# Delta-rule step: reordering the products with the state and sharing one PSUM bank between outputs and update

## The chip, the cores and the metric

The kernel runs on one core of one Trainium2 chip. The metric is the device time in microseconds of one execution; the number given for a kernel is the median of its runs.

## What is computed

The reference is two blocks of two transformer layers each, on 512 tokens of 1024 features, the second block with 256 context tokens beside them. The first layer of the second block has, next to an attention with low-rank keys and values (MLA), a gated delta-rule recurrence of 8 heads with 64 features each. It goes over chunks of 64 tokens in both directions. The preparation of a chunk gives `u`, `w`, `qk`, `q_dec`, `k_dec` and the decay `g_last`; then the state `s` (64 x 64 for each head) is carried from chunk to chunk:

```
def step(s, inp):
    u_i, w_i, qk_i, qd_i, kd_i, gl_i = inp
    v_new = u_i - jnp.einsum('bhck,bhkv->bhcv', w_i, s)
    o_i = jnp.einsum('bhck,bhkv->bhcv', qd_i, s) + jnp.einsum('bhcs,bhsv->bhcv', qk_i, v_new)
    s = s * gl_i[..., None, None] + jnp.einsum('bhck,bhcv->bhkv', kd_i, v_new)
    return s, o_i
```

All of this is in float32. The sequence has 4 + 8 chunks (context, then tokens), so there are 12 chunks in each of two directions.

## The kernel before, in words

The whole of both blocks is one program for one core. Weights come from DRAM in units of 128 output features, are split into two float32r parts (`hl`, L397) and multiplied in three passes (`mm3`, L411 to L417). That is most of the time and is not touched.

The change lies in the stage marked "gdn" (L1792 to L1818). `gdn_scan` (L1518) runs six walks (`walk`, L1624). A walk calls `solve` (L1524) once for each direction, which prepares a block of 128 tokens (two chunks), and then `step` (L1583) four times: two chunks, and for each both directions in turn. So there are 24 steps. Between the walks, and before the first one, units of the MLA attention are traced (`mla`, L1378, by the counts in `UNITS`, L288): scores `S` (L1400), their maxima and exponentials (`soft_rows`, L1320), transpositions `ptr` (L1346) and products with the values `po` (L1363).

The framework that the kernel is written in orders the instructions of each engine itself: it takes what was traced first among what is ready by its own model, and it writes all semaphores. So the order in the trace is not the order of the source; work of the attention and of the next `solve` fills TensorE's places while a step waits for VectorE. An engine then runs its list strictly in that order. The framework keeps two engines that use one PSUM bank of a tile apart in time.

A step, with `rows` the 64 partitions of its chunk:

- L1586 to L1588: four products `ws` = w times state (`wT`, `St`), into a PSUM tile of the ring "step". This ring has a single bank (`MIXERS`, L289), so every PSUM tile of a step waits until the one before it has been read.
- L1589 and L1590: VectorE makes `vn` = u - ws.
- L1591 to L1597: the outputs `ot`, in a new tile of the same ring. For each of the four pairs of heads one product of the state with `qd` (stationary operand 128 x 128, 64 columns) and then, added to it, one product of `vn` with `qk` for each of the two heads (64 x 64, 64 columns).
- L1598 to L1604: the outputs go to `oT`: ScalarE copies them where this chunk is seen for the first time (L1603), VectorE adds them where the other direction has been there (L1601).
- L1605 to L1608: the update `up`, in a third tile of the ring: eight products of `kd` and `vn` (64 x 64, 64 columns).
- L1609 to L1615: VectorE, for each half of the partitions, multiplies the state by its decay (L1614) and adds the update (L1615).

A float32 product shows in the trace as two matmuls, each with a weight load of its own: 8 for `ws`, 8 and 16 for `ot`, 16 for `up` in each step.

Of the kernel before, what the change touches and what calls it, by code (L numbers as in the profile page):

```python
# [26 lines left out]
class Cols:  # L27
    """Names columns of a packed [128, n] array."""
# [17 lines left out]
def units(w, m=128):  # L46
    """[K, N] -> [N/m, 128, K/128 * m]: one weight unit after the other, each contiguous per partition."""
    k, n = w.shape
    return np.ascontiguousarray(w.reshape(k // 128, 128, n // m, m).transpose(2, 1, 0, 3)).reshape(n // m, 128, -1)


def chunk_units(w, sizes):
    """[K, N], K cut into chunks of sizes*128 -> flat array of units (chunk, n): [128, size*128] each."""
    out, k0 = [], 0
    for s in sizes:
        out.append(units(w[k0:k0 + s * 128]).reshape(-1))
        k0 += s * 128
    return np.concatenate(out)
# [26 lines left out]
def chunk_constants():  # L85
    """Masks of chunks of 64 tokens, two chunks on 128 partitions."""
# [45 lines left out]
def na_bias(rpb):  # L132
    """rpb laid out over [query in block, 256 context keys and the block's local keys]; NEG outside the window."""
# [18 lines left out]
def prepare(x):  # L152
    """Lays the inputs out: feature-major activations, weights in units, vectors as columns."""
# [85 lines left out]
def build(tc, A, out, cst_at, vec_at, chk_at, tap=None, upto=99, mark=lambda n: None):  # L239
# [16 lines left out]
    def store(dst, src):  # L256
        """apart from the loads, which it would hold back while it waits"""
        nc.gpsimd.dma_start(dst, src)
# [48 lines left out]
    # ---- scratch, by block  # L307
# [3 lines left out]
    def scr(tag, cols=512):  # L311
        """nt, sq: for the products; ct, cs: for the norms of parts that run beside"""
        p, w = state["sp"] if tag in ("nt", "sq") else (state["np"], {tag: 256})
        return p.tile([128, w[tag]], F32, name=tag, tag=tag, bufs=2 if tag == "sq" else 3)[:, :cols]
# [14 lines left out]
    # ---- background work: the adaLN products, a unit after each unit of weights  # L329
# [9 lines left out]
    # ---- the norms of a part of the tokens, which go along with the products of the next one  # L339
# [15 lines left out]
    def settle(sl=None):  # L355
        """all that the tokens wait for"""
# [3 lines left out]
    def release():  # L360
        """what reads the last products"""
        while pending and not pending[-1][2]:
            advance()

    # ---- weights: a raw unit, its float32r head and its rest
# [12 lines left out]
    # the units in the order of their use, each made two units before it  # L378
# [3 lines left out]
    def plan(seq):  # L382
        """Units to come: (src, tiles, place or None, key), or the key of a unit made before, which still lies there"""
        coming.extend(seq)
# [16 lines left out]
    # ---- activations in two parts: h(p, k, tokens) is feature tile k of the head (p = 0) or the rest  # L401
# [9 lines left out]
    def mm3(jobs, kt=8, first=True, last=True, k0=0):  # L411
        """jobs: (ps, (H, L), activations, tokens); ps += sum_k W[k]^T h[k0 + k], in three float32r passes, k outermost"""
# [6 lines left out]
    def unit_on(kt, h, sls, src=None):  # L419
        """One unit of weights times the token slices: a bank each."""  # L420
# [7 lines left out]
    def linear(units_, h, sls, groups, evac, skew=0, kt=8, stay=3):  # L428
        """Plans the units, returns the run: evac(i, tokens, ps) for each unit; the first `skew` units go group of parts
        by group, so that a part whose input comes late doesn't hold the others; the last units of a group (stay) serve  # L430
        the next one too"""
# [14 lines left out]
        def early(n):  # L446
            """the products of the first n steps, whose places come later"""
# [14 lines left out]
    def places(p, n, kt=8):  # L462
        """n places for weights that stay, in pool p"""
        return [[p.tile([128, kt, 128], F32R, name=f"keep{i}{q}") for q in "HL"] for i in range(n)]

    def out_linear(srcs, h, parts, evac, after, keep=(), lead=1):
        """Plans the units, returns the run: part by part, all the output tiles: evac(n, tokens, ps), then after(tokens).
        srcs[n]: the units of output tile n along the contraction, [(src, tiles)].
        Units with a place of their own (keep) are made once, as are the last ones of a part for the next part.
        lead: so many output tiles at first go along the contraction together"""  # L470
# [38 lines left out]
    # ---- norms over the features (partitions and tiles)  # L509
    def add_square(acc, v, tag="sq"):  # L510
        """acc[0] (+)= v^2"""
# [9 lines left out]
    def rsqrt_cols(sqs, ns, n, off, ring="ax", p=None):  # L521
        """1/sqrt(sum over 128/ns partitions / n + off): tokens on the partitions, a column for each of their blocks and sums"""
# [10 lines left out]
    def rsqrt_steps(sq, n, out):  # L533
        """rsqrt_bc(sq, 1, n) in steps, appended to out"""
# [4 lines left out]
    def on_features(rs, ns, ws, ring="ax"):  # L539
        """such columns on the partitions of their features again: in PSUM, in parts of the widths ws"""  # L540
# [17 lines left out]
    def modulated(xk, rs, a, b, h, sl, ks=range(KD)):  # L558
        """h (in two parts) = x * rs * a + b"""
# [7 lines left out]
    # ---- softplus of a small array  # L567
# [16 lines left out]
    # ---- adaLN: products along the free axis, one output feature per partition  # L584
# [22 lines left out]
    # ======== block 1 ========  # L607
# [15 lines left out]
    def x_plus(gate, acc):  # L623
        """x[n] += gate[n] * ps, and the squares of the sum"""
# [36 lines left out]
    # ---- layer 0: RG-LRU  # L661
    def rglru(after, acc):
        m = mod[0]
        with ExitStack() as st:
# [7 lines left out]
            def yLt(n, dt=F32R):  # L672
                """the rests of block n of y; other things lie there before"""
# [12 lines left out]
            # the first units go along with the modulation of the feature tiles; weights of some lie where y will be  # L686
# [44 lines left out]
            # the steps, by block of features; the gates' units come late, beside the recurrences  # L731
# [35 lines left out]
            def head(n):  # L767
                """the gates of the recurrence; its input lies where y's rest will be"""
# [49 lines left out]
    # ---- layer 1: DSA  # L818
    def stack(dst, p, v, sl):
        """A pair of heads of 64 features: the head and the rest of each on all partitions, as units 2p and 2p + 1"""  # L820
# [6 lines left out]
    def stacked(ps, q, kHL, sl):  # L827
        """q k of such units: k in two parts, each on both halves of the partitions"""
# [3 lines left out]
    def dsa(h, after, acc):  # L832
        m = mod[1]
        with ExitStack() as st:
# [34 lines left out]
            def evac(i, sl, ps):  # L869
# [22 lines left out]
                else:  # L892
# [3 lines left out]
                    # 1 / sqrt(64 (mean square + eps)): the norm and the scale of the scores  # L896
# [6 lines left out]
            def index(b):  # L903
                """the 128 best keys of each query of block b"""
# [35 lines left out]
            def weights(b, g, Ps):  # L940
                """the softmax of the heads of group g, query block b"""
# [52 lines left out]
            def o(p, k, sl):  # L994
                """the output lies where its queries were"""
# [35 lines left out]
    def chain(name, g, sc, sh):  # L1031
        """The next norm's input, made part by part as x is finished."""
# [41 lines left out]
    # ======== block 2 ========  # L1074
# [18 lines left out]
    def grid(v, n=8):  # L1093
        """tokens row by row of the grid, as (row, column) of a tile that goes column by column"""
# [11 lines left out]
    def decay_logs(stack):  # L1106
        """lg: log decay and log beta; egc, kdw: exp of the decays' sums along the chunks, from both ends"""
# [25 lines left out]
    # ---- the products of the even mixer's input: all that the mixers need goes to DRAM  # L1133
    def even_in(h, beside):
        """beside: called after the products that it needs, returns functions to run one by one between the others"""
        with ExitStack() as st:
# [73 lines left out]
            def conv(i):  # L1210
# [23 lines left out]
                # the norms of some units together, for the sake of the tables of functions  # L1234
# [17 lines left out]
            def stored(i, c):  # L1252
                """tokens on the partitions"""
# [65 lines left out]
    # ---- softmax over the free axis, and the products with the values  # L1319
    def soft_rows(Ps, scores, scale, mx, rsum):  # L1320
        """P = exp(scale * (S - max S)), and its sums; scores(i): S of row i in PSUM, in pieces side by side"""
# [13 lines left out]
    def weigh(po, Ps, keys, vals, tp, ring):  # L1335
        """po[64 * half:, (i, q)] = sum over key tiles j of V^T P[half][i]^T; keys[j]: the keys of each i, [(first, number)];
        vals(half, j): V, or V for each i"""
# [84 lines left out]
    def off_diagonal(d, a):  # L1422
        """rows and columns of the block of NT off the diagonal, of chunk a"""
# [4 lines left out]
    def gdn_chunks(gp, slots):  # L1428
        """The inverses of the chunks' triangles, q k with decays to DRAM: a list of functions to run in order.
        slots: 7 tiles of [128, 32, 32]"""  # L1430
# [13 lines left out]
        def decays(b):  # L1444
            """NT[s, h, c] = k_s k_c beta_s decay(s -> c) within chunks, and q_c k_s likewise, of both directions"""
# [43 lines left out]
        def triangles(key, A):  # L1489
            """1 + A = the transpose of a diagonal 32-block of 1 + N, or itself, so that A is an upper triangle;  # L1490
            every block on its own partition."""
# [4 lines left out]
        def invert(key, A, X, Y):  # L1496
            """Y: the inverses, with the row of the block on the partitions, the block of tokens on their quadrant"""
# [20 lines left out]
    def gdn_scan(oT, gA, gp, beside, then):  # L1518
# [5 lines left out]
        def solve(d, b):  # L1524
            """u = T v, w = T (k exp(g)) of both chunks of a block of 128 tokens; T beta is the chunk's inverse"""
# [13 lines left out]
            # the block off the diagonal, of the inverse of [[1 + N1, 0], [N, 1 + N2]]: -(1 + N2)^-1 N (1 + N1)^-1, transposed  # L1539
# [43 lines left out]
        def step(d, b, a, St):  # L1583
# [7 lines left out]
            po = bank("step", 256, "ot")  # L1591
            for p in range(4):
                o = po[:, 64 * p:64 * p + 64]
                T.matmul(o, St[:, p], qd[:, p, rows], start=True, stop=False)  # L1594
                for half in range(2):
                    h = 2 * p + half
                    T.matmul(o[64 * half:64 * half + 64], vn[rows, h], qk[rows, 64 * h:64 * h + 64], start=False, stop=True)  # L1597
# [7 lines left out]
            pu = bank("step", 256, "up")  # L1605
            for h in range(8):
# [551 lines left out]
```

## Time and profile before

| | us |
|---|---|
| timed runs | 3346.09, 3351.06, 3357.49 |
| median of the runs | 3351.06 |
| span of the profiled execution, first to last instruction | 3335.9 |
| TensorE busy in it | 3192.8 (96%) |
| VectorE busy in it | 2066.5 (62%) |
| ScalarE busy in it | 1470.4 (44%) |
| gdn stage in it, about | 1545 to 1895 from the start |

The profiled execution has a span alone; what lies around it is read from the median, 3351.06 - 3335.9 = 15.2 us. In all tables PE is TensorE's matmuls, PEld its weight loads, DVE VectorE, ACT ScalarE, POOL GpSimd, SP the queue of the DMAs. "x16" is a count of instructions. L1608 is a line of the kernel. In a timeline, successive instructions of one kind are merged in one row; its duration goes to the modelled end of the last, so what a run takes of TensorE's time is read from its start to the next row's start.

### The profile page before, as it was taken

How to read it: one execution, taken by the hardware profiler on the slowest of the kernel's cores; microseconds unless marked ns; L12 is line 12 of the kernel's file. 1: busy time of each engine (PE TensorE's matmuls, PEld its weight loads, DVE VectorE, ACT ScalarE, POOL GpSimd, SP SyncE). 2: the span in 40 equal slices, each digit the busy share in tenths (PEclk: the TensorE clock that was granted, in tenths of full speed). 3: DMA queues.
4: the chain of work that ended last, by engine and by line, in shares of the span. 5: the costliest groups of instructions: out<-in, count | busy, mean ns of one | idle time of the engine just before them, and what ended most of it. 6: DMA issues, size and time to landing. Idle time of an engine off the chain costs nothing.

```text
span 3335.9 us, 50730 instructions
## 1 busy us (share of the span) xinstructions
PE 3192.8 (96%) x20270; PEld 2686.0 (81%) x20270; DVE 2066.5 (62%) x4067; ACT 1470.4 (44%) x2638; POOL 17.4 (1%) x47
## 2 busy tenths in 40 slices
PE   6999999989999999988999999999997999999998
PEld 5788888965988889866677799888887877798887
DVE  7976555798787787677756575442228446573335
ACT  4955333457443335476343463212125445563222
POOL 0000000000000000000000000000000000000000
PEclk9999999989999999998889999999998999999999
DMA  7556664310365554333122333532213221143323
GB/s 237 183 156 211 194 190 157 107 51 26 103 212 192 190 198 135 117 127 107 48 64 82 105 108 108 158 127 84 68 62 117 84 89 44 58 139 103 99 97 102
DMA packets 137614, 403.58 MB, mean 121 GB/s; under 512 B 13856, under 2 KB 37152, under 8 KB 136736
## 3 DMA queue, kind: packets, MB, share of 16 engines
q1 hardware_dynamic: 135344, 389.32, 36.5%
q0 software_dynamic: 2032, 11.01, 1.0%
q8 instruction: 159, 2.61, 0.3%
q14 instruction: 79, 0.65, 0.1%
HBM read 375.63 MB, written 24.64 MB: 120 GB/s over the span
## 4 chain that ended last, share of the span: by engine, by line
PE 71%; DVE 6%; ACT 3%; issue 1%; DMA 0%; DVEq 0%; ACTq 0%
PE mm L416 51%; PE ptr L1346 2%; PE po L1363 2%; PE rb L547 2%; PE S L1400 2%; PE S L830 1%; PE ss L527 1%; PE ot L1594 1%; PE ot L1597 1%; PE sa L1560 1%; PE ws L1588 1%; PE po L969 1%; ACT wH L398 1%; PE ptr L975 1%; DVE acc L519 1%
## 5 line engine op out<-in xcount | busy, mean ns | idle before, releaser
L398 ACT CAST wH<-raw 128x1024 fp32r<-128x1024 f32 (+4 forms) x446 | 451.9, 1015 | 1149.7 <-PE mm L416 797.9
L399 DVE TENSOR_TENSOR wL<-raw,wH 128x1024 fp32r<-128x1024 f32 (+4 forms) x446 | 525.0, 1179 | 372.6 <-ACT wH L398 365.8
L416 PE MATMUL mm<-mH,wH 128*128 128x256 f32 (+1 forms) x1280 | 407.3, 340 | 9.1 <-DVE f L1747 5.9
L416 PE MATMUL mm<-mH,wL 128*128 128x256 f32 (+1 forms) x1280 | 404.6, 339 | 1.4 <-DVE wL L399 1.4
L416 PE MATMUL mm<-mL,wH 128*128 128x256 f32 (+1 forms) x1280 | 404.8, 339 | 0.0
L589 DVE SCALAR_TENSOR_TENSOR raw<-raw,cond_c 128x1024 f32<-128x1024 f32 x128 | 156.5, 1224 | 176.2 <-DMA raw<-in_ada 175.7
L416 PEld LDWEIGHTS mm<-mH,wH 128*128 128x128 f32 x1280 | 231.3, 190 | 40.2 <-ACT wH L398 6.6
L416 PEld LDWEIGHTS mm<-mH,wL 128*128 128x128 f32 x1280 | 230.4, 190 | 30.4 <-DVE wL L399 1.8
L416 PEld LDWEIGHTS mm<-mL,wH 128*128 128x128 f32 x1280 | 230.9, 190 | 28.5
L416 PE MATMUL mm<-f2u0L,wH 128*128 128x512 f32 (+1 forms) x752 | 190.3, 327 | 0.0
L416 PE MATMUL mm<-f2u0H,wH 128*128 128x512 f32 (+1 forms) x752 | 190.0, 326 | 0.0
L416 PE MATMUL mm<-f2u0H,wL 128*128 128x512 f32 (+1 forms) x752 | 189.6, 326 | 0.0
L416 PE MATMUL mm<-f2u1H,wL 128*128 128x512 f32 (+1 forms) x432 | 151.4, 352 | 1.2 <-DVE wL L399 1.1
L416 PE MATMUL mm<-f2u1H,wH 128*128 128x512 f32 (+1 forms) x432 | 150.9, 352 | 0.6 <-ACT nt L1722 0.5
L416 PE MATMUL mm<-f2u1L,wH 128*128 128x512 f32 (+1 forms) x432 | 151.2, 352 | 0.2
L416 PEld LDWEIGHTS mm<-f2u0H,wL 128*128 128x128 f32 x752 | 118.1, 189 | 13.1
L416 PEld LDWEIGHTS mm<-f2u0H,wH 128*128 128x128 f32 x752 | 117.7, 189 | 12.9
L416 PEld LDWEIGHTS mm<-f2u0L,wH 128*128 128x128 f32 x752 | 117.7, 189 | 12.6
L1727 DVE TENSOR_TENSOR nt<-nt,mm 128x512 f32<-128x512 f32 (+1 forms) x52 | 31.4, 605 | 145.9 <-PE mm L416 145.5
L626 DVE SCALAR_TENSOR_TENSOR x<-mm,mod,x 128x256 f32<-128x256 f32 (+1 forms) x112 | 66.0, 596 | 78.7 <-PE mm L416 78.5
L416 PE MATMUL mm<-f0H,wH 128*128 128x512 f32 (+1 forms) x296 | 107.2, 363 | 0.0
L416 PE MATMUL mm<-f0L,wH 128*128 128x512 f32 (+1 forms) x296 | 107.0, 362 | 0.0
(692 smaller groups left out, 7488.2 us busy)
## 6 DMA issues: line engine op xcount, KB each, us to landing
raw<-in_ada SPq DMA_DIRECT2D x192, 512.0 KB, 3.7
raw<-in_fw SPq DMA_DIRECT2D x142, 512.0 KB, 4.2
raw<-in_gw SPq DMA_DIRECT2D x113, 512.0 KB, 3.3
raw<-in_gw SPq DMA_DIRECT2D x34, 384.0 KB, 3.0
raw<-in_owin SPq DMA_DIRECT2D x25, 512.0 KB, 3.3
raw<-in_ewin SPq DMA_DIRECT2D x22, 512.0 KB, 3.5
raw<-in_awin SPq DMA_DIRECT2D x20, 512.0 KB, 3.7
raw<-in_ewout SPq DMA_DIRECT2D x18, 512.0 KB, 4.1
```

What stands on the lines that cost most here:

```text
L398: S.copy(H, src)
L399: V.tensor_tensor(L, src, H.bitcast(F32), OP.subtract)
L416: T.matmul(ps, W[w][:, k], h(p, k0 + k, sl), start=first and k == 0 and j == 0, stop=last and k == kt - 1 and j == 2)
L519: V.tensor_tensor(acc[0], acc[0], sq, OP.add)
L527: T.matmul(pc[:, ns * b:ns * b + ns], sq, sel, start=True, stop=True)
L547: T.matmul(pb[r * i:r * i + r, b:b + 128], rs[:, c:c + 1].to_broadcast([128, r]), ident, start=True, stop=True)
L589: V.scalar_tensor_tensor(junk, r, 1.0, c, OP.mult, OP.mult, accum_out=o[:, j:j + 1])
L626: V.scalar_tensor_tensor(x[:, n, sl], ps, gate[:, n:n + 1], x[:, n, sl], OP.mult, OP.add)
L830: T.matmul(ps, q, k[:, sl], start=j == 0, stop=j == 1)
L1346: T.transpose(pt[:kn, c:c + 128], Ps[half][i][:, k0:k0 + kn], ident)
L1363: T.matmul(po[r], vs, PT[:kn, half * w:half * w + w], start=j == 0, stop=j == len(keys) - 1)
L1400: T.matmul(pS, q, KQ[half][:, 0, k0 + c0:k0 + c1], start=True, stop=True)
```

## The change

Within `step`, `ot` and `up` become one tile `ou` of the ring "step": its first 256 columns are `po`, the last 256 `pu`. Its 20 products follow one another: the four of the state and `qd`; the eight of the update; the eight of `qk`. A first product alone has the start flag, which clears the bank for all of them. The outputs are read after the last product, and the two operations of VectorE on the state follow as before. The rest of the diff removes comments and docstrings.

```diff
             vn = gp.tile([128, 8, 64], F32, name="vn", bufs=3)
             V.tensor_tensor(vn[rows], u[rows], pw[rows].rearrange("p (h c) -> p h c", h=8), OP.subtract)
-            po = bank("step", 256, "ot")
+
+            ou = bank("step", 512, "ou")
+            po, pu = ou[:, :256], ou[:, 256:]
             for p in range(4):
-                o = po[:, 64 * p:64 * p + 64]
-                T.matmul(o, St[:, p], qd[:, p, rows], start=True, stop=False)
-                for half in range(2):
-                    h = 2 * p + half
-                    T.matmul(o[64 * half:64 * half + 64], vn[rows, h], qk[rows, 64 * h:64 * h + 64], start=False, stop=True)
+                T.matmul(po[:, 64 * p:64 * p + 64], St[:, p], qd[:, p, rows], start=p == 0, stop=False)
+            for h in range(8):
+                r = slice(64 * (h % 2), 64 * (h % 2) + 64)
+                T.matmul(pu[r, 64 * (h // 2):64 * (h // 2) + 64], kd[rows, h], vn[rows, h], start=False, stop=False)
+            for h in range(8):
+                r = slice(64 * (h % 2), 64 * (h % 2) + 64)
+                T.matmul(po[r, 64 * (h // 2):64 * (h // 2) + 64], vn[rows, h], qk[rows, 64 * h:64 * h + 64],
+                         start=False, stop=h > 5)
             ot = oT[:, :, 128 * b + 64 * a:128 * b + 64 * a + 64]
             o3 = po.rearrange("p (i t) -> p i t", i=4)
             if (b, a) in seen:
...
                 S.copy(ot, o3)
                 seen.add((b, a))
-            pu = bank("step", 256, "up")
-            for h in range(8):
-                r = slice(64 * (h % 2), 64 * (h % 2) + 64)
-                T.matmul(pu[r, 64 * (h // 2):64 * (h // 2) + 64], kd[rows, h], vn[rows, h], start=True, stop=True)
             last = 64 * a + (63 if d == 0 else 0)
             p3 = pu.rearrange("p (i t) -> p i t", i=4)
             for half in range(2):
```

## Rows read from the trace of the kernel before

**Rows 1.** The chain that ended last, by line, from 1500 to 2100 us.
```profile
by line: PE mm L416 30.4%; PE S L1400 9.8%; PE po L1363 6.1%; PE ptr L1346 6.0%; PE ot L1594 5.7%; PE ot L1597 4.6%; PE sa L1560 4.2%; PE ws L1588 4.2%; PE rb L547 2.9%; PE up L1608 2.9%; PE gg L1550 2.5%; PE nd L1547 2.4%; PE eg L1573 1.9%
```

**Rows 2.** Busy time of each engine by stretch; the stage is the last row.
```profile
core 0: us, PE busy (x) PEld busy (x) DVE busy (x) ACT busy (x) POOL busy (x), PEclk, DMA share, GB/s
1545.00:1600.00 55.00, 51.21 (x478) 38.89 (x478) 38.30 (x124) 28.79 (x61) 0.71 (x2) 0.83 0.24 75
...
1650.00:1700.00 50.00, 46.91 (x348) 31.70 (x348) 27.96 (x73) 21.71 (x43) 1.07 (x2) 0.66 0.16 42
1700.00:1750.00 50.00, 50.00 (x458) 37.09 (x456) 25.90 (x72) 21.77 (x47) 1.64 (x3) 0.90 0.25 70
...
1800.00:1850.00 50.00, 50.00 (x513) 37.60 (x513) 26.06 (x71) 16.70 (x40) 0.56 (x1) 0.97 0.10 30
1850.00:1900.00 50.00, 47.28 (x409) 32.99 (x407) 26.80 (x64) 16.32 (x29) 1.09 (x2) 0.97 0.29 101
1545.00:1900.00 355.00, 342.07 (x3154) 247.50 (x3154) 214.49 (x595) 145.66 (x307) 8.82 (x17) 0.89 0.23 70
```

**Rows 3.** Timeline of TensorE: the products of one step, from 1732 us.
```profile
1732.44 0.43 PE L1594 MATMUL ot<-qd,St 128*128 128x64 f32 x2
1732.80 0.33 PE L1597 MATMUL ot<-qk,vn 64*64 64x64 f32 x4
1733.06 0.43 PE L1594 MATMUL ot<-qd,St 128*128 128x64 f32 x2
...
1734.94 0.43 PE L547 MATMUL rb<-cst,rsum 128*64 128x128 f32 x2
...
1736.37 0.68 PE L1608 MATMUL up<-vn,kd 64*64 64x64 f32 x16
1736.98 0.66 PE L1346 MATMUL ptr<-cst,P 128*128 128x128 f32 x4
```

**Rows 4.** The same timeline: runs of 128x128 stationary operands, and 512-column products.
```profile
1738.19 1.12 PE L1400 MATMUL S<-kq 96*128 96x512 f32 x2
1739.24 0.69 PE L1550 MATMUL gg<-DT,ND 32*32 32x32 f32 x16
...
1743.10 1.38 PE L1560 MATMUL sa<-VK,DT 128*128 128x128 f32 x10
1744.32 0.95 PE L527 MATMUL ss<-cst,sq 128*128 128x2 f32 x8
1745.13 0.42 PE L1566 MATMUL wt<-cst,w__15727 128*128 128x128 f32 x2
```

**Rows 5.** Waits at line L1608: what ended TensorE's idle time before it.
```profile
  issue: 3.6, 10
  DVE St L1614: 2.8, 4
  ACT oT L1603: 1.4, 3
```

**Rows 6.** VectorE's group of the state's decay, 1545 to 1895 us; its idle time last.
```profile
L1614 DVE TENSOR_TENSOR St<-St,eb 64x256 f32<-64x256 f32 x48 | 20.1, 419 | 39.1 <-PE ot L1594 38.3
```

**Rows 7.** The two readers of the outputs: durations (min/median/max, ns) and counts.
```profile
L1601 DVE TENSOR_TENSOR oT<-ot,oT x12: 386/410/425, 1638.1 to 1878.7; 128x256 f32<-128x256 f32 x12
L1603 ACT COPY oT<-ot x12: 367/372/373, 1570.4 to 1786.1; 128x256 f32<-128x256 f32 x12
```

**Rows 8.** Line L1563, ScalarE's reads of a bank that VectorE reads too: its waits.
```profile
  DVE u L1562: 17.4, 16
```

**Rows 9.** Timeline, all engines: the end of updates and the start of a next step.
```profile
1650.07 0.43 DVE L1615 TENSOR_TENSOR St<-up,St 64x256 f32<-64x256 f32 x1
...
1650.61 0.97 PEld L1588 LDWEIGHTS ws<-St,wT 128*64 128x64 f32 x8
...
1737.10 0.88 DVE L1615 TENSOR_TENSOR St<-up,St 64x256 f32<-64x256 f32 x2 [0.19 <-PE up L1608]
```

**Rows 10.** TensorE's group of `ws`, 1545 to 1895 us; its idle time last.
```profile
L1588 PE MATMUL ws<-St,wT 128*64 128x128 f32 x192 | 30.0, 303 | 1.3 <-DVE St L1615 1.1
```

## The prediction

> **What bounds the kernel now.** I read the chain of waits first, for the 600 us around the changed code [rows 1]. It runs almost wholly over TensorE, and the three lines of the step that the change touches hold 5.7 + 4.6 + 2.9 = 13.2% of it, about 79 us. The reader should see that the chain goes through these products at every step, so time saved in them is on the path as long as TensorE stays the engine that ends the stage. Next the busy time by stretch [rows 2]: in the stage of 355 us TensorE is idle for 13 us; from 1700 to 1850 us it has no idle time (two of the three slices stand in the rows; the third reads the same), while VectorE is busy for half of it and ScalarE for less. Before 1700 there are holes of 3 to 4 us in a slice of 50. The granted clock is 0.89 over the stage, a mixture of 2.4 and 1.2 GHz, lowest (0.66) in 1650 to 1700. So this is a TensorE-bound stage with a step chain threaded through it, and the questions are how much of TensorE's time the new order gives back, and whether the single PSUM bank of the step makes a new wait.
>
> **The change, part by part.**
>
> *Order of the products.* Today the 8 matmuls on `qd` and the 16 on `qk` alternate, 2 and 4 at a time, in four rounds. In a step without a hole at full clock [rows 3] they take 1732.44 to 1734.94 = 2.50 us. A round is 0.36 us for two `qd` matmuls up to the start of the next row, and 0.26 for four `qk` matmuls. The update, 16 matmuls of the same small form, takes 1736.37 to 1736.98 = 0.61 us. Four small ones cost 0.26, sixteen cost 0.61: each costs (0.61 - 0.26) / 12 = 0.029, and leaving the run costs 0.26 - 4 x 0.029 = 0.14. Each round pays this exit, and the update pays it once more. After the change 32 small matmuls stand in one run: 32 x 0.029 + 0.14 = 1.07 us.
>
> For eight `qd` matmuls in one run the trace has no row. The nearest is `sa`, with the same 128 x 128 stationary operand: ten in 1743.10 to 1744.32, so 0.122 us each [rows 4]. I take 8 x 0.122 = 0.98 us. Its moving operand is 128 columns and not 64, so it should rather be too dear. The bound below is `ss`, with 2 columns: eight in 0.81 us, 0.101 each. The bound above is that nothing is gained: 4 x 0.36 = 1.44 us.
>
> Together a step's products behind `vn` cost 2.50 + 0.61 = 3.11 us now and 0.98 + 1.07 = 2.05 after: 1.06 us less. With 24 steps that is 25.4 us at full clock, and at the stage's mean clock of 0.89 about 28.5 us. With the bounds: 24 x (3.11 - 2.51) / 0.89 = 16 us, and 24 x (3.11 - 1.88) / 0.89 = 33 us.
>
> *One PSUM tile fewer.* The update no longer waits for the outputs to be read. TensorE's loads sat idle before L1608 for 3.6, 2.8 and 1.4 us in the largest three entries [rows 5], 7.8 us in all. Part of this is only the loads, behind matmuls still running. I take 0 for it and keep 8 us as the further bound.
>
> *Waits moved.* The multiplication of the state by its decay (L1614) needs the last `qd` product. Today that stands near the end of `ot`, and VectorE sits 39 us idle in front of it [rows 6]; in the new order it is free after 1 us and lies beside the 1.07 us of small products (two operations of 0.42). Cost 0; if it came late it would delay the adds by 0.84. The adds (L1615) now wait for the last `qk` product and for the reader of the outputs, since the bank is shared. In 12 steps this reader is VectorE itself, ahead of them in its queue; in the other 12 it is ScalarE's copy of 0.37 us [rows 7]. While VectorE waits there, the attention's maxima and its copies of `ptr` queue behind, and TensorE's `ptr` and `po` wait for those. Twelve waits of 0.4 us are 5 us of an engine that has 355 - 214 = 140 us idle [rows 2]. I take 0; without that cover it is 5 us.
>
> *Rest.* Matmuls, weight loads and VectorE operations keep their number. No DMA is issued, removed or moved past another, on SP or POOL. The start and stop flags cost nothing.
>
> *Sum.* The profiled execution has a span of 3335.9 us and lies 15.2 us under the median of the runs. 3335.9 - 28 = 3308 of span, plus 15.2: **3323 us**.
>
> **The rivals.**
>
> *The freed time is lost to other waits.* TensorE holds no slack in 1700 to 1850, and little after, but the first nine steps (before 1711 us) lie where it already waits for VectorE and ScalarE. If only the fifteen steps after them gain, it is 15 x 1.06 = 16 us, about 3335, still faster. If the attention's softmax keeps its pace in the whole stage, the gain goes to idle time there, and it comes out at 3345 to 3351. Against it: VectorE is half idle in 1700 to 1850.
>
> *The end of a step lies bare: slower.* The 20 products leave one gap at their end. From the last product to the next `ws` there stand, in a row, the hand-over (0.05: the update of rows 3 ended at 1737.05, the add began at 1737.10 [rows 9]), the outputs' reader (0.37 to 0.41 [rows 7]), a second hand-over, the two adds (0.88), and the return to TensorE (1650.50 to 1650.61, 0.11 [rows 9]): 1.48 us. Before, the reader's time lay under other work between `ot` and `up`. If the list has nothing ready there, 24 x 1.48 = 36 us of holes stand against 28 gained, +8. Holes bring the clock down too: the slice 1650 to 1700, with 3 us idle, was granted 0.66 [rows 2], a loss of 0.34 x 50 = 17 us; one more such slice makes it +25, 3376 us. It decides once about four of five ends lie bare (28 / 36). Against it: `ws` waits today behind a chain of 1.0 us (the adds and both hand-overs), and TensorE idled only 1.3 us before all 24 of them [rows 10].
>
> The Trainium skill, "PSUM — Partial Sum Buffer", PSUM bank collisions, is the rule behind this rival: two engines may not touch one bank and quadrant at once, reads against reads included. The trace agrees: ScalarE's copy of half a bank waited 16 times, 17.4 us, for VectorE's read of the other half [rows 8].
>
> *Grouping `qd` gains little.* If the load of each `qd` matmul and its stream of columns come one after the other even in a run, each costs 0.101 (the load, from `ss`) plus 64 columns; two `S` matmuls of 512 columns took 1.05 us [rows 4], so 64 columns are 0.066 and eight matmuls 1.34 us. The step then saves 3.11 - 1.34 - 1.07 = 0.70 us, in all 24 x 0.70 / 0.89 = 19 us, 3332. Against it: `sa`, with 128 columns, would by this cost 0.101 + 0.131 = 0.23 each, and its row says 0.122. The Trainium skill, "TensorE: Matmul & The Clock Gate", Part 3, The mechanism, states what would make it so: a weight load overlaps a running matmul only where the two lie on different row groups, and all `qd` matmuls use all rows. The row of `sa` differs from that rule.
>
> *More than the sum.* The stage at 0.89 loses 0.11 x 355 = 39 us to the clock. Fewer holes and fewer partly filled runs could give half of it back: 3304.
>
> *The change does not do what it says.* The framework may put other work between the products of `ou`, and TensorE then pays the exits again. Half of the gain, 3337, at best no change.
>
> **How the numbers follow.** About 0.3%, 10 us, is what a measurement of this kernel can tell from no change. The forecast (22 to 41 us less) gets 0.44; more by the clock 0.12; the `qd` matmuls with load and stream apart 0.06; the gain from the later steps alone, 3335, or half the gain by other work in between, 0.13: all faster, 0.75. All of it lost to other waits, or undone by the order, 0.15: the same. The bare ends 0.10: slower. The range goes from 3303, below the sum with the upper bounds (3351 - 41 = 3310) and at the clock's case, to 3349, within the lost gain; outside lie most of the slower case and a little at either end.
>
> **What would show it.** Right: in the profile after, a step's `ou` products in one block of about 2.05 us at full clock, `qd` rows of 8 and a small run of 32; VectorE's idle time before the decay far below 39 us; the three lines' share of the chain down by about a third; the stage about 28 us shorter, and everything behind it earlier by as much. Wrong: `qd` rows with 0.18 us a matmul; idle time before `ws` of over 20 us, ended by L1615 or its like; a granted clock under 0.85 over the stage; or a stage just as long, with more idle time before `ptr` and `S`.

## The result, and the profile after

The changed kernel takes 3293.32 us in the median of 4 runs (3290.66 to 3293.5), the kernel before 3353.9 in 4 runs of the same comparison. The ratio is 0.9832, with a 95% interval of 0.9818 to 0.9847: 60.6 us less, where 28 was forecast.

The span of the profiled execution fell from 3335.9 to 3291.6 us, by 44.3. Its own time is 3293.5, so 1.9 us lie around the span, not 15.2.

The step in the new order, in the changed kernel's timeline of all engines (lines have moved: L1595 is `qd`, L1598 the update, L1601 `qk`, L1606 and L1608 the readers of the outputs, L1615 and L1616 the state's decay and add):

```profile
1787.33 1.00 PE L1595 MATMUL ou<-qd,St 128*128 128x64 f32 x8
...
1788.26 0.68 PE L1598 MATMUL ou<-vn,kd 64*64 64x64 f32 x16
1788.37 0.87 DVE L1615 TENSOR_TENSOR St<-St,eb 64x256 f32<-64x256 f32 x2 [2.04 <-PE ou L1595]
...
1788.78 0.63 PE L1601 MATMUL ou<-qk,vn 64*64 64x64 f32 x16
...
1789.34 0.33 PE L1346 MATMUL ptr<-cst,P 128*128 128x128 f32 x1
...
1790.33 0.87 DVE L1616 TENSOR_TENSOR St<-ou,St 64x256 f32<-64x256 f32 x2
```

Twenty products stand in one block of 1787.33 to 1789.34 = 2.01 us, where [rows 3] has 2.50 and 0.61. The decay (L1615) lies beside the small products.

The changed kernel's groups of TensorE and of VectorE, 1545 to 1855 us (busy us, mean ns, then the idle time before them):

```profile
L1588 PE MATMUL ws<-St,wT 128*64 128x128 f32 x192 | 29.0, 295 | 4.3 <-DVE St L1616 4.2
L1595 PE MATMUL ou<-qd,St 128*128 128x64 f32 x192 | 27.0, 284 | 0.2 <-DVE vn L1590 0.2
```

```profile
L1615 DVE TENSOR_TENSOR St<-St,eb 64x256 f32<-64x256 f32 x48 | 20.1, 418 | 18.9 <-PE ou L1595 18.0
L1616 DVE TENSOR_TENSOR St<-ou,St 64x256 f32<-64x256 f32 x48 | 20.1, 418 | 1.7 <-ACT oT L1608 1.0
```

VectorE's idle time before the decay halved, 39.1 [rows 6] to 18.9. The wait at the end of a step is there, and small: TensorE idles 4.3 us before the 24 `ws`, against 1.3 [rows 10], and VectorE waited 1.0 us for ScalarE's reading of the shared bank.

The same stretches of the changed kernel as in [rows 2]:

```profile
1545.00:1600.00 55.00, 49.90 (x483) 39.90 (x481) 38.33 (x121) 27.91 (x60) 0.00 (x0) 0.75 0.24 72
1650.00:1700.00 50.00, 47.36 (x458) 34.71 (x456) 33.70 (x86) 26.88 (x53) 1.59 (x3) 0.86 0.27 73
1700.00:1750.00 50.00, 49.19 (x574) 37.73 (x572) 33.06 (x88) 28.22 (x61) 1.12 (x2) 1.00 0.30 103
1800.00:1850.00 50.00, 47.23 (x476) 33.84 (x478) 31.92 (x83) 21.91 (x44) 0.55 (x1) 1.00 0.24 80
```

TensorE has no fewer holes. What rose is the granted clock: 0.66 to 0.86 in the slice from 1650, 0.90 to 1.00 in the next; in the first slice it fell, from 0.83 to 0.75.

To part the two, I take the stage from the first `ws` to the first `ss` behind it (where the next stage begins), once for the kernel before and once for the changed one, by the view of busy time by stretch:

```profile
1557.73:1894.09 336.36, 326.17 (x2987) 233.31 (x2984) 204.66 (x570) 132.06 (x283) 8.09 (x15) 0.89 0.21 65
```

```profile
1560.01:1853.19 293.18, 281.77 (x2987) 208.47 (x2985) 203.33 (x570) 131.30 (x284) 8.10 (x15) 0.95 0.24 75
```

The stage is 43.2 us shorter, so it holds all but 1 us of the difference of the spans. Length times granted clock is the time that it would take at 2.4 GHz throughout: 336.4 x 0.89 = 299 us before, 293.2 x 0.95 = 279 after (to about 1.7 us, since the clock has two digits). The rest of the length is lost to the low clock: 37 us before, 15 after. So of 43 us about 20 are TensorE's own time and about 22 are clock. TensorE's idle time is 336.36 - 326.17 = 10.2 us before and 11.4 after, so holes don't explain the clock.

### The profile page after: what moved, and what is told of

Same layout as the page of the kernel before. It is cut to its first block, busy times and chain, and to the rows that moved or that the text cites. A ratio compares the mean times of both kernels' runs of the same rounds, so it can differ in the third digit from the quotient of the medians.

```text
span 3291.6 us, 50721 instructions
## 1 busy us (share of the span) xinstructions
PE 3147.9 (96%) x20270; PEld 2659.1 (81%) x20270; DVE 2065.0 (63%) x4067; ACT 1468.9 (45%) x2638; POOL 17.4 (1%) x47
## 4 chain that ended last, share of the span: by engine, by line
PE 69%; DVE 6%; ACT 4%; issue 1%; DMA 0%; SPq 0%; DVEq 0%; ACTq 0%
PE mm L416 51%; PE ptr L1346 2%; PE po L1363 2%; PE rb L547 2%; PE S L1400 1%; PE S L830 1%; PE ss L527 1%; PE ws L1588 1%; ACT wH L398 1%; PE po L969 1%; PE ou L1595 1%; DVE wL L399 1%; DVE acc L519 1%; PE ptr L975 1%; PE sa L1560 1%
## 5 line engine op out<-in xcount | busy, mean ns | idle before, releaser
L416 PEld LDWEIGHTS mm<-mL,wH 128*128 128x128 f32 x1280 | 230.2, 189 | 28.5
```

Source lines behind the costliest of these rows:

```text
L416: T.matmul(ps, W[w][:, k], h(p, k0 + k, sl), start=first and k == 0 and j == 0, stop=last and k == kt - 1 and j == 2)
```

## The experiments

All were compared with the kernel before in the same job. The table uses the stage and the arithmetic above; "lost" is length minus full-clock time. Rows of the stretches behind it stand below, where a verdict rests on them.

The stage's columns come from one trace each. The last two columns do the same sum for the whole program over all timed runs, since a span and a granted clock are on record for each: span times clock, and what is left of the span, medians in us (a run's clock has three digits, which is 1.7 us).

| kernel | median us | ratio to before (95%) | stage us | at full clock | lost | program at full clock | lost |
|---|---|---|---|---|---|---|---|
| before, first trace | 3353.9 | 1 | 336.4 | 299 | 37 | - | - |
| before again | 3347.08 | 1.0005 (0.9991 to 1.002) | 344.3 | 300 | 45 | 3218 | 127 |
| one bank, alternating | 3328.86 | 0.9941 (0.9919 to 0.9963) | 331.2 | 295 | 36 | 3217 | 110 |
| grouped, two banks | 3304.78 | 0.9871 (0.9848 to 0.9894) | 308.8 | 284 | 25 | 3204 | 99 |
| changed kernel | 3293.32 | 0.9832 (0.9818 to 0.9847) | 293.2 | 279 | 15 | 3200 | 90 |
| changed kernel again | 3289.94 | 0.9845 (0.9818 to 0.9871) | 288.0 | 279 | 9 | 3201 | 87 |
| update last | 3286.65 | 0.9819 (0.9794 to 0.9845) | 288.8 | 280 | 9 | 3202 | 82 |
| adds first | 3291.56 | 0.9848 (0.9824 to 0.9872) | 291.9 | 280 | 12 | 3202 | 87 |
| before, fewer columns | 3361.18 | 1.0035 (1.0019 to 1.005) | 366.9 | 290 | 77 | 3210 | 148 |
| before, more columns | 3324.41 | 0.9945 (0.993 to 0.996) | 323.0 | 307 | 16 | 3232 | 93 |
| grouped, two banks, more columns | 3287.87 | 0.9819 (0.9796 to 0.9841) | 289.8 | 284 | 6 | 3207 | 81 |
| attention in pairs | 3280.1 | 0.9816 (0.9791 to 0.984) | 289.8 | 275 | 15 | 3195 | 82 |
| both lowest together | 3285.16 | 0.9808 (0.9786 to 0.9829) | 283.3 | 280 | 3 | 3201 | 85 |

The kernel before, which ran beside each of them, has 3218 and 127 us in the job of experiments 1 to 4, 3221 and 124 in that of 5 to 8, 3221 and 127 in that of 9 to 11. So the change took 18 to 20 us of full-clock time and about 37 us of clock (124 to 87, and 127 to 90 across jobs).

**1. The kernel before again**, unchanged.

> The kernel before, unchanged, profiled and timed once more. Theory A (the profiled execution of before was a lucky one, with a higher granted clock than its timed ones): this trace has its own time near 3352, a span near 3350, and the 14 us against the first trace stand as more time at the low clock. Theory B (the profile's span leaves 15 us around the program): own time minus span is again near 15 us.

Its profiled execution took 3343.24 us with a span of 3341.5: 1.7 us around the span, so theory B falls. The first trace's execution was then near 3335.9 + 2 = 3338 us, at the low end of the 18 runs of this job (3334.08 to 3361.16). The second trace's stage:

```profile
1557.84:1902.18 344.34, 334.00 (x2987) 237.59 (x2984) 205.05 (x570) 132.46 (x283) 8.09 (x15) 0.87 0.20 63
```

It is 8 us longer than the first one's at the same full-clock time. Theory A has the cause but not the amount for this trace (3343, not 3352). Over the runs the time goes with the clock granted in the whole program: 3334.08 us at 0.966, 3361.16 at 0.958. Span times clock is the same for both, 3219 and 3218 us. The runs of the changed kernel lie within 3 us, at 0.972 to 0.973.

**2. Grouped, two banks: the order of the products alone.**

```diff
-                o = po[:, 64 * p:64 * p + 64]
-                T.matmul(o, St[:, p], qd[:, p, rows], start=True, stop=False)
-                for half in range(2):
-                    h = 2 * p + half
-                    T.matmul(o[64 * half:64 * half + 64], vn[rows, h], qk[rows, 64 * h:64 * h + 64], start=False, stop=True)
+                T.matmul(po[:, 64 * p:64 * p + 64], St[:, p], qd[:, p, rows], start=p == 0, stop=False)
+            for h in range(8):
+                r = slice(64 * (h % 2), 64 * (h % 2) + 64)
+                T.matmul(po[r, 64 * (h // 2):64 * (h // 2) + 64], vn[rows, h], qk[rows, 64 * h:64 * h + 64],
+                         start=False, stop=h > 5)
```

> The outputs' products grouped (4 on qd, then 8 on qk), the update still in a tile of its own after the outputs are read. Theory A (TensorE's own time falls by the grouping, the clock follows from it): ot takes about 17 us less of full-clock time than before, up stays; stage about 17 to 35 us shorter, time near 3310 to 3330. Theory B (the removed wait between outputs and update gives the gain, the clock's part above all): the low clock stays near 70 us in the stage, and the gain is 17 us at most, near 3335.

41.6 us less than before, with the wait between outputs and update left in place:

```profile
1559.28:1868.05 308.77, 296.65 (x2987) 216.03 (x2984) 206.06 (x570) 132.57 (x283) 8.07 (x15) 0.92 0.23 70
```

The full-clock time fell by 15 to 16 us (17 expected), and the low clock fell too, from 37 to 45 us lost to 25. Over the timed runs it is 14 us of full-clock time (3218 to 3204) and 28 of clock (127 to 99). Theory A holds; theory B's 70 us at the low clock (35 lost) and 17 us at most do not.

**3. One bank, alternating: the removed wait alone.** `ot` and `up` become the tile `ou` as in the change, the update's eight products follow the outputs' twelve, and the loop over `p` keeps its order:

```diff
-            po = bank("step", 256, "ot")
+            ou = bank("step", 512, "ou")
+            po, pu = ou[:, :256], ou[:, 256:]
...
-                T.matmul(o, St[:, p], qd[:, p, rows], start=True, stop=False)
+                T.matmul(o, St[:, p], qd[:, p, rows], start=p == 0, stop=False)
```

> One bank for outputs and update, the update's products right after the outputs', but qd and qk products alternate as before. Theory A: only one exit from a run of small products is saved in each step, 24 x 0.14 = 3 us, and the time stays within 10 us of before. Theory B: the wait is gone, so the low clock in the stage falls from 72 to about 27 us and the time by 20 us or more, near 3325.

17.6 us less in the median. The profiled execution is 3328.86, the median itself:

```profile
1556.99:1888.14 331.15, 321.45 (x2987) 231.66 (x2984) 203.94 (x570) 132.41 (x284) 8.10 (x15) 0.89 0.21 66
```

In the stage of this one trace, full-clock time is down by 4 to 5 us, nearly theory A's 3, and the clock is that of the first trace of before (0.89), so theory B's fall of the low clock to 27 us isn't in it. The timed runs say where the 17.6 us went: full-clock time is 3217 us against 3218, and the loss 110 against 127. Nearly all of it is clock. So the time that theory B expected came for the most part, which A didn't expect: one bank for both results, with the update right behind the outputs, raises the clock also without the grouping. The stage's idle time is 331.15 - 321.45 = 9.7 us, hardly less than the 10.2 of before, so it doesn't say why.

**4. Update last.** The changed kernel with the loop over `qk` ahead of the loop over `kd`.

```diff
+            for h in range(8):
+                r = slice(64 * (h % 2), 64 * (h % 2) + 64)
+                T.matmul(po[r, 64 * (h // 2):64 * (h // 2) + 64], vn[rows, h], qk[rows, 64 * h:64 * h + 64],
+                         start=False, stop=False)
             for h in range(8):
                 r = slice(64 * (h % 2), 64 * (h % 2) + 64)
-                T.matmul(pu[r, 64 * (h // 2):64 * (h // 2) + 64], kd[rows, h], vn[rows, h], start=False, stop=False)
-            for h in range(8):
...
+                T.matmul(pu[r, 64 * (h // 2):64 * (h // 2) + 64], kd[rows, h], vn[rows, h], start=False, stop=h > 5)
```

> The changed kernel with the eight qk products ahead of the eight of the update. Both theories: the same time as the changed kernel within 5 us (3288 to 3298), since the runs of small products are as long and all readers wait for the last product of the bank.

3286.65 us, just below the band; the interval of its ratio (0.9794 to 0.9845) holds the changed kernel's 0.9832. No difference that these runs can tell.

**5. Adds first.** The changed kernel with the reading of the outputs traced behind the state's decay and add (the block from `ot = oT[...]` to `seen.add((b, a))` moves to the end of `step`).

```diff
-            ot = oT[:, :, 128 * b + 64 * a:128 * b + 64 * a + 64]
...
                 V.tensor_tensor(s3, p3[r], s3, OP.add)
+            ot = oT[:, :, 128 * b + 64 * a:128 * b + 64 * a + 64]
...
```

> The changed kernel with the state's two operations traced ahead of the reading of the outputs, so that the adds don't wait for that reader. Theory A (TensorE's own time and its clock decide, the chain's last wait is covered): the same as the changed kernel, 3288 to 3298. Theory B (the shorter chain from one step to the next gives the gain): some 24 x 0.4 = 10 us less, about 3283.

3291.56 us against 3289.94 of the changed kernel in the same job. Theory B's 10 us didn't come, but the edit hardly shortened the chain:

```profile
L1588 PE MATMUL ws<-St,wT 128*64 128x128 f32 x192 | 27.5, 285 | 3.5 <-DVE oT L1613 2.7 <-DVE eo L1505 0.5
```

The next `ws` needs the step's single bank, and now waits for the outputs' reader (L1613) in place of the adds: 3.5 us in all, 4.3 before the edit. What a truly shorter chain would bring isn't shown; at this place it could give back the 4.3 us.

**6. Attention in pairs: another change of form, elsewhere.**

```diff
-            PT = tp.tile([128, 2 * w], F32, name="PT", bufs=3)
+            PT = tp.tile([128, 2 * w], F32, name="PT", bufs=4)
...
-            if j > 1:
+            if j > 2 and j % 2:
                 times(*todo.pop(0))
+                times(*todo.pop(0))
```

> The changed kernel, and in the attentions beside it and in the odd layer two transposed tiles are made before the two products with the values, so that TensorE changes between these two forms half as often (one buffer PT more). Theory A (a change of form costs TensorE time wherever it is): in the stage 28 pairs of changes become 14, each of about 0.3 us, so 4 us less of full-clock time; as much or more in the odd layer; time 3280 to 3290. Theory B (the gain belongs to the step's chain alone): no change, or slower by later products, 3290 to 3305.

3280.1 us (3275.91 to 3286.16), where the changed kernel had 3288.25 to 3292.05 in this job: 10 us less, at theory A's edge, and the lowest median of the study. Over the runs some 6 us of it are full-clock time (3201 to 3195) and 5 are clock (87 to 82). In the stage's one trace the full-clock time is about 4 us less, as expected, and the low clock took that back (289.8 us against 288.0); but experiment 9, with the same attention, has 280 us there. Outside the stage the span fell from 3289.6 - 288.0 = 3001.6 to 3276.5 - 289.8 = 2986.7 us. The edit reaches the odd layer's attention there; the traces were not parted further. Theory A is likely, not shown.

**7. The changed kernel again**, unchanged.

> The changed kernel once more, for a second trace and for the other runs of this job. Both theories: 3287 to 3297; low clock in the stage 15 to 40 us, full-clock time of the stage 279 to 281 us.

```profile
1559.37:1847.34 287.97, 277.07 (x2987) 202.82 (x2985) 203.39 (x570) 131.30 (x284) 8.09 (x15) 0.97 0.24 76
```

As expected: 3289.94 us, full-clock time 279, and 9 us lost, so about 17 at the low clock.

**8. More columns: the cause of the clock.** The kernel before, but each `qd` product runs over both chunks' columns, of which one chunk's are read.

```diff
-            po = bank("step", 256, "ot")
+            po = bank("step", 512, "ot")
             for p in range(4):
-                o = po[:, 64 * p:64 * p + 64]
-                T.matmul(o, St[:, p], qd[:, p, rows], start=True, stop=False)
+                o = po[:, 128 * p:128 * p + 128]
+                T.matmul(o, St[:, p], qd[:, p], start=True, stop=False)
...
-                    T.matmul(o[64 * half:64 * half + 64], vn[rows, h], qk[rows, 64 * h:64 * h + 64], start=False, stop=True)
+                    T.matmul(o[64 * half:64 * half + 64, rows], vn[rows, h], qk[rows, 64 * h:64 * h + 64], start=False, stop=True)
```

> The kernel before with the old order and two banks, but each product on qd goes over 128 columns in place of 64; the 64 columns of the other chunk are left unread. TensorE has 24 x 4 products more columns and no wait less. Theory A1 (the clock falls because the old order streams little): the stage's full-clock time rises by 0 to 10 us, and the low clock in the stage falls from 72 to 88 us to under 50, so the time stays the same or falls, 3325 to 3350. Theory A2 (the clock follows from the waits of the step, which stay): low clock 70 us or more, time 3346 to 3360.

More work, no wait taken out, and 22 us less, 3324.41, just below the band:

```profile
1556.70:1879.73 323.03, 314.40 (x2987) 220.19 (x2985) 205.56 (x570) 132.63 (x284) 8.09 (x15) 0.95 0.22 68
```

The full-clock time rose by 7 us (0 to 10 expected), and the loss to the clock fell from 37 to 45 us to 16 (about 32 at the low level; under 50 expected). Over the timed runs it is 11 us more of full-clock time (3221 to 3232) and 31 less of clock (124 to 93). Theory A1 holds.

**9. Both lowest edits together** (4 and 6).

> The changed kernel with the qk products ahead of the update's and the attentions' tiles in pairs: the two edits that came out lowest, together. If both are real and add up: 3273 to 3282; if the order of the runs of small products was noise: as with the pairs alone, 3276 to 3286.

3285.16 us (3278.47 to 3289.58) at a ratio of 0.9808; with the pairs alone it was 0.9816. The intervals (0.9786 to 0.9829, 0.9791 to 0.984) lie over one another, so no gain of experiment 4's order can be told. The full-clock time is that of the changed kernel, 3201 us: the 6 us that the pairs took off it in experiment 6 aren't seen here.

**10. More columns in the grouped order.** Experiment 2 with the `qd` products over 128 columns.

```diff
-                T.matmul(po[:, 64 * p:64 * p + 64], St[:, p], qd[:, p, rows], start=p == 0, stop=False)
+                T.matmul(po[:, 128 * p:128 * p + 128], St[:, p], qd[:, p], start=p == 0, stop=False)
...
-                T.matmul(po[r, 64 * (h // 2):64 * (h // 2) + 64], vn[rows, h], qk[rows, 64 * h:64 * h + 64],
+                T.matmul(po[r, c:c + 64], vn[rows, h], qk[rows, 64 * h:64 * h + 64],
```

Here `c` is `128 * (h // 2) + 64 * a`.

> The grouped outputs in a bank of their own (3305 us, full-clock time of the stage 283 us, low clock 51 us), with each qd product over 128 columns, half of them unread. Theory A1 (streamed columns keep the clock up): full-clock time 283 to 290, low clock under 35 us, time 3288 to 3302. Theory A2 (the clock follows the waits or only the forms): low clock 45 us or more, time 3305 to 3315.

3287.87 us, ratio 0.9819 against 0.9871 of experiment 2. The outputs still stand in a bank of their own, and the time is that of the changed kernel:

```profile
1556.09:1845.87 289.78, 281.94 (x2987) 205.11 (x2985) 204.03 (x570) 131.73 (x283) 8.10 (x15) 0.98 0.23 71
```

A1 again: the stage's full-clock time stays at 284, and the loss falls from 25 us to 6; over the timed runs from 99 to 81.

**11. Fewer columns.** The kernel before with `qd` products of 8 columns in a place that nobody reads.

```diff
-            po = bank("step", 256, "ot")
+            po = bank("step", 512, "ot")
...
-                T.matmul(o, St[:, p], qd[:, p, rows], start=True, stop=False)
+                T.matmul(po[:, 256 + 64 * p:256 + 64 * p + 8], St[:, p], qd[:, p, 64 * a:64 * a + 8], start=True, stop=True)
...
-                    T.matmul(o[64 * half:64 * half + 64], vn[rows, h], qk[rows, 64 * h:64 * h + 64], start=False, stop=True)
+                    T.matmul(o[64 * half:64 * half + 64], vn[rows, h], qk[rows, 64 * h:64 * h + 64], start=True, stop=True)
```

> The kernel before with each qd product over 8 columns in place of 64, in columns that nobody reads: the state's part of the outputs is left out. TensorE streams less and waits as before. Theory A1: full-clock time of the stage 0 to 10 us lower, low clock above the 72 to 88 us of before, time 3340 to 3365 although less is computed. Theory A2: low clock unchanged, time lower by the full-clock time, 3335 to 3345.

Less work, and slower: 3361.18 us against 3353.07 of the kernel before in this job.

```profile
1564.40:1931.29 366.89, 357.17 (x2987) 255.72 (x2984) 204.22 (x570) 132.03 (x284) 8.09 (x15) 0.79 0.18 56
```

The full-clock time is 10 us lower, and 77 us are lost to the clock. (This execution took 3371.27, ten above the median of its runs, so the loss is at its high end.) With 8, 64 and 128 columns the loss is 77, 37 to 45, and 16 us, in one order of products with no wait taken out; over the timed runs of the whole program 148, 124 to 127, and 93. That the waits alone set the clock (A2) is out. That they have a part in it isn't: in experiment 3 the columns stayed and the loss fell too. Nor do columns per time, taken over the stage, order the losses: by the shapes in the traces it streams 317,472 columns before and 306,720 with fewer, about 1,060 per us at full clock in both, at 37 to 45 and 77 us lost. One reserve: the framework moved some neighbouring work when the columns changed, so the instruction lists of 8, 10 and 11 differ in places from those they are compared with.

## Why the prediction was right and wrong

**Right: the time of the products.** The forecast was 25.4 us of full-clock time; the stage lost 20 (299 to 279), the program 18 to 20 in the timed runs. Of the 5 us between, about 3 are TensorE's longer wait before `ws` (4.3 us against 1.3), which the sum put at nothing. The block has 2.01 us, 2.05 were forecast; the run of eight `qd` matmuls has 1787.33 to 1788.26 = 0.93, 0.98 were forecast. That is 0.116 us each, and the rival that keeps each load and its stream apart (0.167) is out: the Trainium skill's rule on row groups ("TensorE: Matmul & The Clock Gate", Part 3, The mechanism) doesn't describe this run. The same section of the Trainium skill has a second case, a load into the background weight buffer, that would let loads run ahead; no run here shows whether it is this one. By the prediction's rows the grouping of the outputs was to give 24 x (2.50 - 0.98 - 0.60) = 22 us and the update beside them 24 x 0.14 = 3; the stages of experiments 2 and 3 have 15 to 16 and 4 to 5, the timed runs 14 and 1.

**Wrong: the clock.** The step that failed is "at the stage's mean clock of 0.89 about 28.5 us". It divided the gain by the clock of the old order as though the clock belonged to the stage. It belongs to the order: the change took the stage's loss from 37 us in the first trace of before, 45 in the second, to 15 and 9. That is a second gain of 22 to 36 us, as large as the first; in the timed runs of the whole program it is about 37. Both halves of the change have a share: the grouping alone took 28 us off the loss (experiment 2), the one bank alone 17 (experiment 3). The rival "more than the sum" had this, with half of 39 us given back, and was held at 0.12. Its reason was half right: not "fewer holes", as TensorE's idle time is 10 to 11 us in both kernels. With it goes the price of the bare ends' "one more such slice": the idle time rose from 10.2 to 11.4 us and the clock from 0.89 to 0.95. The other half, "fewer partly filled runs", fits: more columns on the `qd` products raise the clock (experiments 8, 10, 11). That grouping and the shared bank raise it in the same way is argued, not shown.

**Wrong: the base.** "Lies 15.2 us under the median" took all of this for time around the span. Only 2 us are; the other 13 came from an execution of before that was quicker than most. Against the median of the first comparison it is 3353.9 - 3338 = 16 us, so 16 of the 60.6 are in no difference of the first two traces; 44 are, 20 + 22 of them as above. By other runs of the same kernel these 16 are clock too: in experiment 1's job a run of 3338.12 us has a span of 3336.4 at 0.965, one of 3353.3 a span of 3351.5 at 0.960, which is 3220 and 3217 us at full clock. For the first comparison's own runs of before no clock is on record.

**Right: the waits.** The bare end of the step, the slower rival, is there with 4.3 us before `ws`, far from the 36 that it needed. Its rule, "PSUM — Partial Sum Buffer", PSUM bank collisions raise a hardware error, in the Trainium skill, fits what the trace has: VectorE's add did wait for ScalarE's reading of the shared bank, once, for 1.0 us. The framework writes that wait, so the trace can't show what the chip would do without it. Experiment 5 took this order away and gained nothing, since the bank's reader still stands before the next `ws`. VectorE's cover held.

**The lost-time rival** fell: the stage got shorter by more than TensorE's time, and the attention kept pace. That the order might not come out as written fell with the timeline: the eight `qd` matmuls stand in one run in 21 of the 24 steps.

## What to carry to other kernels

Where TensorE bounds a stage at a granted clock below 1, an edit to the order of its products can change the clock as well as their time. Give the clock a term of its own in the forecast, with a range, and don't divide by the clock of the old order: grouping equal forms paid twice here, 14 us for the products and 28 in the clock (experiment 2). Length times granted clock parts the two. Do it over all timed runs: in experiment 3 one trace gave 5 us to the products, and seven runs gave them 1 and the clock 17. A variant with idle extra columns tests whether the clock is in play. Before working out a difference from one trace, place that execution among the timed runs.

## What the runs showed of the hardware

More work made the kernel faster. With 64 unread columns more on each of 96 products the kernel before went from 3346.87 to 3324.41 us, and its stage from a granted clock of 0.87 to 0.89 up to 0.95; with 56 fewer it went to 0.79 and the kernel from 3353.07 to 3361.18. TensorE was busy for 97% of the stage in each (326.17 of 336.36, 314.40 of 323.03, 357.17 of 366.89 us), so the busy share doesn't tell which of the two clock levels is granted.

A TensorE run of small products costs more than its products. Four `qk` matmuls took 0.26 us and the update's sixteen 0.61, each with another form behind them [rows 3], so four cost well over a quarter of sixteen. In the changed kernel's block the update's sixteen took 0.52 with a run of the same form behind them (1788.26 to 1788.78), and the sixteen `qk` 0.56 with another form behind (1788.78 to 1789.34).
